# A hybrid two-layer diffusion step on one core: where a group's first weighted sum stands in its tick, and when the second layer's tables are asked for

## The chip, the cores and the metric

The kernel runs on one core of a Trainium2 chip. The metric is the device time of one execution in microseconds (us), the median of several runs. PE is TensorE, DVE VectorE, ACT ScalarE, POOL GpSimd; SP issues the transfers (DMAs).

## The reference

One step of a backbone with two layers over 1024 latent tokens and 256 context tokens of width 1024. What bears on this case:

```python
# layer 0: windowed grouped-query attention (16 heads of 64, 4 key/value heads) beside an mLSTM
q_block: p = softmax([q.k_window + mask, q.k_cache, sink])       # blocks of 128 queries
         o = p_window @ v_window + p_cache @ v_cache
out  = concat(o * silu(za), h_mlstm * silu(zb)) @ w_out_ab
# layer 1: latent attention (16 heads)
qa, kva, kr, z = split(h @ w_in_c)                                # widths 384, 256, 32, 1024
q = rmsnorm(qa) @ w_qb;  kv = concat(rmsnorm(kva), cache_c_kv) @ w_kvb
kr = concat(axial_rope(kr), cache_c_krope)
out = (softmax(q.k) @ v * silu(z)) @ w_out_c
```

Every layer is wrapped in RMSNorm, shift, scale, gate and a residual sum.

## The kernel before

All products run as three float32r matmuls each (high by high, high by low, low by high), so every operand is split by a cast (ACT) and a difference (DVE or POOL). The token axis is cut into 10 tiles of 128 (8 latent, 2 context).

**The windowed attention of layer 0.** `Attention.run` writes the order of the work out by hand, tick by tick, and the engines keep it. The work is 40 groups: 4 key/value heads times 10 query blocks, four query heads each. A group has 2 to 5 blocks of keys, and each block takes one tick of `use`: `turn` transposes the four heads' probabilities on PE into a bank of `mm`, `split` casts them to `att_ph` (ACT) and takes the rest `att_pl` (DVE), and one tick later `weighted` (from line 1041 of the loop) multiplies both with the values into the bank `V`. There is one bank of this kind (`K.set_psum(D=2, mm=3, V=1)`); the first `weighted` of a group (`k == 0`) takes it anew. After the last one, `out` reads it: two ACT instructions (L1145, L1146) and two on DVE (L1147, L1148), all into `att_o`. In the same ticks `scores` computes another group's scores into `D`, `peak` takes their maximum on DVE (L1103, L1104), `exp` the exponentials on ACT (L1109), and `normal` scales them on POOL (L1118).

In between, `extra(i)` fills PE with other work: at first the last projection block, and from tick 26 on steps of the output projection of layer 0 (`out_steps`), three matmuls `mm<-w,o_ah`/`o_al` a step. Up to tick 55 there is a step in every third tick, after that at least one in nearly every tick, sometimes two:

```python
while i > n + 8 and left > (160 - (i - n - 8) / 3 if i < n + 39 else 150 * (A.end - i) / (A.end - n - 39)):
    next(steps)
```

The stretch with a step in every third tick is called the thin part below, the rest the dense part.

**The start of layer 1.** `layer_c` is outside that hand-written order: a scheduler places its instructions on each engine by their dependences. `dense` holds the blocks of the projection `h @ w_in_c`: one block of `z`, two of `u` (the columns of `qa`, `kva` and `kr`), three more of `z`. A block's weights come in four transfers `wf` of two slices each (`DenseBlock.ask`, two buffers), are cast to `wh` (L353, ACT) and subtracted to `wl` (L354, POOL). A `z` block passes each result through `silu2_out` (L644 ACT, L645 DVE into `sz_th`), and SP stores it to `csz`. The `u` results are copied by ACT (L1772). The tables are `rtab` (named `rtabc` in the trace: rotary cosine and sine, 128x2048, 1 MB) and `cc` (the cached latents, 256 and 32 KB): `k_rope` and the later `rope` calls read the first, `k_rope(K, 3)` and transposes after the projection the second. `wq` (2304 KB) is asked for behind `dense.run(2)`.

All transfers stand in one queue, SP's. An issue that waits holds up those behind it.

**The latent attention** (`Mla`) follows, in which POOL forms a small product (L2123) and scales three pieces of the probabilities (L2128) for each block of queries.

Of the kernel before, what the change touches and what calls it, by code (L numbers as in the profile page):

```python
# [143 lines left out]
def body(tc, I, O, dbg=None, stop_at=None):  # L144
    K = Kern(tc, I, O, dbg)
    with ExitStack() as ctx:
        K.const = ctx.enter_context(tc.tile_pool(name="const", bufs=1))
        K.dram = ctx.enter_context(tc.tile_pool(name="dram", bufs=1, space=DRAM))
        K.left = lambda n: tc.alloc_tile_pool(name=n, bufs=1, side="left", reuse_waits="tile")
        K.right = lambda n: tc.alloc_tile_pool(name=n, bufs=1, side="right", reuse_waits="tile")  # L150
        K.set_psum(S=6, T=2)
        setup_consts(K)
        layer_ab(K)
        layer_c(K)
        K.set_psum()
# [176 lines left out]
class DenseBlock:  # L332
# [31 lines left out]
    def run(self):  # L364

        units = self.fn(self.w)
        if self.K.pairs:
            for half in range(2):
                for u in units[0:2]:
                    u.products(half, 2)  # L370
                    yield u.cost / 2
            units = units[2:]
        for u in units:
            n = u.cost if self.K.pairs else 2 * u.cost
            for i in range(n):
                u.products(i, n)
                yield u.cost / n
# [48 lines left out]
class Dense:  # L426
# [30 lines left out]
    def pump(self, now):  # L457

        if not self.blocks:
            return  # L460
        b = self.blocks[0]
        if b.asked < KD // 2 and len(b.wf) < 2:
            b.ask()
            b.when.append(now + 3)
        if b.wf and len(b.w) < 2 * b.bufs - KD and now >= b.when[0]:
            b.when.pop(0)
            b.split()
# [500 lines left out]
class Attention:  # L968
# [51 lines left out]
    def run(self, pump, extra):  # L1020

        K, flow = self.K, self.K.flow
        for i in range(self.end + 5):
            flow.now += 1
            pump(flow.now)
            for f in self.ask.get(i, ()):
                f()
            if i - 2 in self.score:
                G, h = self.score[i - 2]
                if h % 2:  # L1030
                    G.normal(h // 2)
            if i - 1 in self.score:
                G, h = self.score[i - 1]
                G.peak(h)
            if i in self.use:
                G, k = self.use[i]
                G.turn(k)
                G.split(k)
            if i - 1 in self.use:
                G, k = self.use[i - 1]  # L1040
                G.weighted(k)
                if k == len(G.kbs) - 1:
                    G.out()
            if i - 1 in self.score:
                G, h = self.score[i - 1]
                G.exp(h)
            flow.step()
            extra(i)
            if i in self.score:
                G, h = self.score[i]  # L1050
                G.scores(h)
# [777 lines left out]
def layer_c(K):  # L1829
# [10 lines left out]
    K.cc = cu.tile([128, 2, 288], F32, tag="cc", name="cc")  # L1840
    K.u = [cu.tile([128, 672], F32, tag=f"u{t}", name=f"u{t}") for t in range(NT)]
    dense = Dense(K.cblocks)
    dense.run(1)
    K.dma(K.rtab, I["k_ropec"].rearrange("p (a t) -> p a t", a=2))
    K.dma(K.cc[:, :, 0:256], I["cache_c_kv"][0, 0].rearrange("(a p) f -> p a f", p=128))
    K.dma(K.cc[:, :, 256:288], I["cache_c_krope"][0, 0].rearrange("(a p) f -> p a f", p=128))
    ncol = cu.tile([128, 5], F32, tag="ncol", name="ncol")
    ps = K.psT()
    K.tr(ps[:, 0:5], qnr)
# [397 lines left out]
```

## Time and profile before

| | us |
|---|---|
| runs | 2660.78, 2662.75, 2665.32 |
| median | 2662.75 |
| profiled execution, its time | 2661.53 |
| its span, first to last instruction | 2659.5 |
| PE busy | 2584.5 (97%) |
| DVE, ACT, POOL busy | 1775.5, 1409.0, 1167.7 |
| granted PE clock, mean | 0.992 |

The profile is of one execution. A row of a timeline has the start in us from the span's start and the length; what stands in brackets at its end is the engine's idle time before it, with the instruction that ended it. Matmuls overlap, so the length of one is longer than the distance to the next; what the engine really loses at a place is read from starts.

### The profile page before, as it was taken

The page shows a single profiled execution, that of the slowest core. Times are in us where ns is not written, and L with a number is a line of the kernel's source. Part 1 is how long each engine was busy: PE and PEld are TensorE (multiplying, and loading weights), DVE is VectorE, ACT ScalarE, POOL GpSimd, SP SyncE. Part 2 cuts the span into 40 slices and gives each one's busy share as a digit, 9 for nine tenths or more (in the row PEclk, how much of TensorE's full clock was granted, in tenths as well). Part 3 has the DMA queues.
Part 4 walks back from the last instruction along what each step waited for, and adds up shares of the span by engine and source line. Part 5 has one row for each costly group of instructions (what it writes and reads, how often), then busy time and mean ns, then how long its engine had stood idle before and what let it go on. Part 6 is the DMA issues. An engine that isn't in the chain of part 4 may idle for free. (4 is left out here: it accounts for less than half of the span.)

```text
span 2659.5 us, 48212 instructions
## 1 busy us (share of the span) xinstructions
PE 2584.5 (97%) x16209; PEld 2264.8 (85%) x16209; DVE 1775.5 (67%) x4040; ACT 1409.0 (53%) x3598; POOL 1167.7 (44%) x1533
## 2 busy tenths in 40 slices
PE   8989999999999999989999999999999999999998
PEld 6778898898998888877888878987799999999886
DVE  6883565756747566487777545334788888888853
ACT  5222444534533433386666533323688888888842
POOL 5343333523424444275545453223455545555632
PEclk9989999999999999999999999999999999999999
DMA  7555556556657655463433463433311101100333
GB/s 248 177 156 158 161 180 198 170 167 202 203 173 222 204 173 177 150 190 104 129 102 110 128 197 117 132 92 111 104 30 33 39 30 39 37 21 27 123 104 127
DMA packets 344585, 348.79 MB, mean 131 GB/s; under 512 B 29609, under 2 KB 291414, under 8 KB 344082
## 3 DMA queue, kind: packets, MB, share of 16 engines
q1 hardware_dynamic: 344338, 345.71, 42.5%
q8 instruction: 129, 2.11, 0.3%
q14 instruction: 118, 0.97, 0.1%
HBM read 235.09 MB, written 110.51 MB: 130 GB/s over the span
## 5 line engine op out<-in xcount | busy, mean ns | idle before, releaser
L354 POOL TENSOR_TENSOR wl<-wf,wh 128x256 fp32r<-128x256 f32 (+2 forms) x288 | 251.7, 899 | 455.0 <-ACT wh L353 385.1
L103 PE MATMUL mm<-hTh,wh 128*128 128x512 f32 (+1 forms) x912 | 328.3, 360 | 1.6 <-DVE scr L620 0.9
L103 PE MATMUL mm<-hTl,wh 128*128 128x512 f32 (+1 forms) x912 | 325.1, 356 | 0.0
L103 PE MATMUL mm<-hTh,wl 128*128 128x512 f32 (+1 forms) x912 | 325.0, 356 | 0.0
L103 PE MATMUL S<-cK,cQ 96*128 96x512 f32 (+3 forms) x1248 | 297.9, 364 | 3.1 <-ACT cPb L2149 2.0
L2197 DVE TENSOR_TENSOR cpl<-T,cph 128x512 fp32r<-128x512 f32 x336 | 228.4, 685 | 38.8 <-ACT cph L2196 35.2
L103 PEld LDWEIGHTS S<-cK,cQ 96*128 96x128 f32 (+1 forms) x1248 | 192.0, 189 | 26.9 <-ACT cPb L2149 4.8
L2196 ACT CAST cph<-T 128x512 fp32r<-128x512 f32 x336 | 192.6, 590 | 27.6 <-PE T L107 15.3
L103 PEld LDWEIGHTS mm<-hTh,wl 128*128 128x128 f32 x912 | 171.8, 188 | 26.6
L103 PEld LDWEIGHTS mm<-hTh,wh 128*128 128x128 f32 x912 | 171.5, 188 | 25.9 <-DVE bmod L306 1.7
L103 PEld LDWEIGHTS mm<-hTl,wh 128*128 128x128 f32 x912 | 171.6, 188 | 23.1
L2147 DVE TENSOR_REDUCE cmx<-S 128x1 f32<-128x512 f32 x256 | 173.0, 681 | 17.1 <-PE S L103 15.5
L103 PE MATMUL V<-cph,cV 128*128 128x256 f32 x672 | 176.7, 289 | 0.0
L103 PE MATMUL V<-cpl,cV 128*128 128x256 f32 x672 | 172.0, 284 | 1.3 <-DVE cst L2121 1.3
L103 PE MATMUL S<-w,o_ah 128*128 128x512 f32 x492 | 151.8, 395 | 1.7 <-POOL w L820 0.8
L2128 POOL TENSOR_SCALAR cPa<-cPa,cst 128x512 f32<-128x512 f32 x128 | 99.4, 776 | 117.3 <-DVE cst L2125 89.3
L103 PE MATMUL mm<-w,o_ah 128*128 128x512 f32 x468 | 148.6, 396 | 0.0
L1129 ACT CAST att_ph<-mm 128x512 fp32r<-128x512 f32 x168 | 98.6, 587 | 93.8 <-PE mm L107 92.5
L1118 POOL TENSOR_SCALAR att_p<-att_p,att_den 128x640 f32<-128x640 f32 (+1 forms) x128 | 97.5, 775 | 108.9 <-DVE att_den L1115 47.9
L353 ACT CAST wh<-wf 128x256 fp32r<-128x256 f32 (+2 forms) x288 | 102.2, 410 | 70.2 <-DMA wf<-in_w_in_ab 32.4
L1130 DVE TENSOR_TENSOR att_pl<-mm,att_ph 128x512 fp32r<-128x512 f32 x168 | 115.8, 689 | 33.1 <-ACT att_ph L1129 27.9
L103 PE MATMUL mm<-wh,hTh 128*128 128x256 f32 x480 | 135.6, 283 | 0.0
(432 smaller groups left out, 7832.5 us busy)
## 6 DMA issues: line engine op xcount, KB each, us to landing
wf<-in_w_in_ab SPq DMA_DIRECT2D x120, 256.0 KB
in<-in SPq DMA_DIRECT2D x40, 514.0 KB
in<-in SPq DMA_DIRECT2D x32, 386.0 KB
mw<-in_w_mod SPq DMA_DIRECT2D x48, 256.0 KB
in<-scr SPq DMA_DIRECT2D x40, 258.0 KB
o_x<-y SPq DMA_DIRECT2D x20, 512.0 KB
wm<-in_w_mod SPq DMA_DIRECT2D x16, 512.0 KB
in<-cx SPq DMA_DIRECT2D x32, 256.0 KB
```

The costliest lines, as they stand in the source:

```text
L103: return self.nc.tensor.matmul(out, lhsT, rhs, start=start, stop=stop)
L353: K.nc.scalar.copy(wh, wf[:, k])
L354: K.nc.gpsimd.tensor_sub(wl, wf[:, k], wh.bitcast(F32))
L1118: nc.gpsimd.tensor_scalar(pv, pv, den[:, i:i + 1], 1.0, ALU.mult, ALU.mult)
L1129: K.nc.scalar.copy(ph, self.T)
L1130: K.nc.vector.tensor_sub(pl, self.T, ph.bitcast(F32))
L2128: nc.gpsimd.tensor_scalar(pv, pv, wt[:, c:c + 1], rd, ALU.mult, ALU.mult)
L2147: nc.vector.tensor_reduce(mx[:, b, c:c + 1], S, AX.X, ALU.max, negate=True)
L2196: nc.scalar.copy(ph, T_)
L2197: nc.vector.tensor_sub(pl, T_, ph.bitcast(F32))
```

## The change

Two places are written in another order; no instruction is added or removed. In `Attention.run` the `weighted` of a group's first key block is called after `extra(i)` instead of before `exp`. In `layer_c` the three transfers of `rtab` and `cc` are asked for before `dense.run(1)`.

```diff
@@ -1038,7 +1038,8 @@
             if i - 1 in self.use:
                 G, k = self.use[i - 1]
-                G.weighted(k)
+                if k:
+                    G.weighted(k)
                 if k == len(G.kbs) - 1:
                     G.out()
             if i - 1 in self.score:
@@ -1046,6 +1047,10 @@
                 G.exp(h)
             flow.step()
             extra(i)
+            if i - 1 in self.use:
+                G, k = self.use[i - 1]
+                if not k:
+                    G.weighted(k)
             if i in self.score:
                 G, h = self.score[i]
                 G.scores(h)
@@ -1840,10 +1845,10 @@
     dense = Dense(K.cblocks)
-    dense.run(1)
     K.dma(K.rtab, I["k_ropec"].rearrange("p (a t) -> p a t", a=2))
     K.dma(K.cc[:, :, 0:256], I["cache_c_kv"][0, 0].rearrange("(a p) f -> p a f", p=128))
     K.dma(K.cc[:, :, 256:288], I["cache_c_krope"][0, 0].rearrange("(a p) f -> p a f", p=128))
+    dense.run(1)
     ncol = cu.tile([128, 5], F32, tag="ncol", name="ncol")
```

PE at one boundary of the dense part, before: `mm` from `att_p` is a transpose, `V` the weighted sum of the new group, `mm` from `w` a step of the output projection, `D` the scores.

```order
L107 MATMUL mm_16844<-small,att_p_16618 128x128 x2
L107 MATMUL mm_16844<-small,att_p_16679 128x128 x2
L103 MATMUL V_16853<-att_ph_16818,att_v 128x512
L103 MATMUL V_16853<-att_pl_16819,att_v 128x512
L103 MATMUL mm_16638<-w_15377,o_ah_16355 128x512
L103 MATMUL mm_16638<-w_15378,o_ah_16355 128x512
L103 MATMUL mm_16638<-w_15377,o_al_16356 128x512
L103 MATMUL D_16861<-att_kh,att_q_16736 128x384
```

The same place in the changed kernel:

```order
L107 MATMUL mm_16844<-small,att_p_16618 128x128 x2
L107 MATMUL mm_16844<-small,att_p_16679 128x128 x2
L103 MATMUL mm_16638<-w_15377,o_ah_16352 128x512
L103 MATMUL mm_16638<-w_15378,o_ah_16352 128x512
L103 MATMUL mm_16638<-w_15377,o_al_16353 128x512
L103 MATMUL V_16858<-att_ph_16818,att_v 128x512
L103 MATMUL V_16858<-att_pl_16819,att_v 128x512
L103 MATMUL D_16861<-att_kh,att_q_16736 128x384
```

The two matmuls of the first weighted sum have moved behind the three of the step; transposes and scores stand where they were. In a tick without a step nothing moves.

SP's queue at the start of layer 1, before (`csz` are stores of the first `z` block, `mw` weights of the modulation, `bmod` its bias):

```order
L138 DMA kvb<-in_kv_norm_c 128x256
L138 DMA csz_4184_19569<-sz_th_20566 128x512
L138 DMA rtabc<-in_k_ropec 128x2048
L138 DMA csz_4185_19570<-sz_th_20595 128x512
L138 DMA cc<-in_cache_c_kv 128x2x256
L138 DMA cc<-in_cache_c_krope 128x2x32
L138 DMA wq<-in_w_qb_c 128x3x1536
L138 DMA mw_21583<-in_w_mod 128x256
L138 DMA wf_20523<-in_w_in_c 128x2x336
L138 DMA csz_4184_19569<-sz_th_20624 128x512
```

The same place in the changed kernel:

```order
L138 DMA kvb<-in_kv_norm_c 128x256
L138 DMA rtabc<-in_k_ropec 128x2048
L138 DMA cc<-in_cache_c_kv 128x2x256
L138 DMA cc<-in_cache_c_krope 128x2x32
L138 DMA csz_4184_19569<-sz_th_20569 128x512
L138 DMA csz_4185_19570<-sz_th_20598 128x512
L138 DMA wq<-in_w_qb_c 128x3x1536
L138 DMA wf_20526<-in_w_in_c 128x2x336
L138 DMA mw_21583<-in_w_mod 128x256
L138 DMA mw_21585<-in_w_mod 128x256
```

The tables stand ahead of the two stores, and the first `wf` one place ahead of the first `mw`; the third store, which stood right behind `wf`, is now behind `bmod`.

ACT at the same place, before (`wh` casts weights, `sz_th` is the first half of the silu, `u` the copy of a projection result):

```order
L353 CAST wh_20515<-wf_20503 128x336
L353 CAST wh_20519<-wf_20503 128x336
L644 ACTIVATE sz_th_20624<-S_20599 128x512
L353 CAST wh_20525<-wf_20513 128x336
L353 CAST wh_20529<-wf_20513 128x336
L644 ACTIVATE sz_th_20653<-S_20628 128x512
L353 CAST wh_20533<-wf_20523 128x336
L353 CAST wh_20537<-wf_20523 128x336
L644 ACTIVATE sz_th_20682<-S_20657 128x256
```

And in the changed kernel:

```order
L353 CAST wh_20518<-wf_20506 128x336
L353 CAST wh_20522<-wf_20506 128x336
L353 CAST wh_20528<-wf_20516 128x336
L353 CAST wh_20532<-wf_20516 128x336
L644 ACTIVATE sz_th_20627<-S_20602 128x512
L644 ACTIVATE sz_th_20656<-S_20631 128x512
L353 CAST wh_20536<-wf_20526 128x336
L353 CAST wh_20540<-wf_20526 128x336
L353 CAST wh_20727<-wf_20723 128x336
```

The casts have moved ahead of the `sz_th` instructions. Farther on, the scheduler places the first part of the latent attention in a somewhat other order on PE, ACT, DVE and POOL; the rest of it stands as before.

## Rows read from the trace of the kernel before

**Rows 1.** The page's head: span and number of instructions, then busy time of each engine with its share of the span.
```profile
span 2659.5 us, 48212 instructions
...
PE 2584.5 (97%) x16209; PEld 2264.8 (85%) x16209; DVE 1775.5 (67%) x4040; ACT 1409.0 (53%) x3598; POOL 1167.7 (44%) x1533
```

**Rows 2.** TensorE's waits in the dense part of the windowed attention, 1215 to 1510 us: who was waited for, us in total, times, longest.
```profile
PE V L103 <- DVE att_o L1148: 4.8, 20, 0.4
```

**Rows 3.** The same view for the thin part, 1110 to 1215 us.
```profile
PE V L103 <- DVE att_o L1148: 7.4, 9, 1.1
```

**Rows 4.** TensorE in order of time in the dense part: start, length, instruction, out<-in, count, and in brackets the idle time before it with what ended it. The transposes write `mm` from `att_p`, the weighted sum writes `V`, the filling products read `w,o_ah`, the scores write `D`.
```profile
1309.85 0.60 PE L107 MATMUL mm<-small,att_p 128*128 128x128 f32 x4
1310.64 0.47 PE L103 MATMUL V<-att_ph,att_v 128*128 128x512 f32 x1 [0.19 <-DVE att_o L1148]
...
1311.18 0.63 PE L103 MATMUL mm<-w,o_ah 128*128 128x512 f32 x2
...
1311.88 0.34 PE L103 MATMUL D<-att_kh,att_q 128*128 128x384 f32 x1
...
1312.65 0.60 PE L107 MATMUL mm<-small,att_p 128*128 128x128 f32 x4
1313.01 0.48 PE L103 MATMUL V<-att_ph,att_v 128*128 128x512 f32 x1
```

**Rows 5.** TensorE's weight loads in order of time, at the same boundary.
```profile
1310.61 0.19 PEld L103 LDWEIGHTS V<-att_ph,att_v 128*128 128x128 f32 x1 [0.40 <-ACT att_p L1109]
```

**Rows 6.** TensorE in order of time, at a boundary behind the last block of a head group's sequence (narrower windows).
```profile
1299.08 0.60 PE L107 MATMUL mm<-small,att_p 128*128 128x128 f32 x4
1300.05 0.47 PE L103 MATMUL V<-att_ph,att_v 128*128 128x512 f32 x1 [0.36 <-DVE att_o L1148]
```

**Rows 7.** VectorE in order of time, at the boundary of rows 4.
```profile
1310.07 0.43 DVE L1148 SCALAR_TENSOR_TENSOR att_o<-V,att_o 64x256 f32<-64x256 f32 x1
1310.53 0.16 DVE L1103 COPY D<-sink 128x1 f32<-128x1 f32 x1
1310.72 0.82 DVE L1104 TENSOR_REDUCE att_nm<-D 128x1 f32<-128x641 f32 x1
1311.47 0.68 DVE L1130 TENSOR_TENSOR att_pl<-mm,att_ph 128x512 fp32r<-128x512 f32 x1
```

**Rows 8.** TensorE in order of time, at a boundary whose tick before holds two steps of products: the second step of that tick, then transposes and weighted sum of the next.
```profile
1421.90 0.62 PE L103 MATMUL mm<-w,o_ah 128*128 128x512 f32 x2
...
1423.36 0.60 PE L107 MATMUL mm<-small,att_p 128*128 128x128 f32 x4
1423.71 0.48 PE L103 MATMUL V<-att_ph,att_v 128*128 128x512 f32 x1
```

**Rows 9.** TensorE in order of time in the thin part: the weighted sums of two boundaries whose tick holds products.
```profile
1154.62 0.47 PE L103 MATMUL V<-att_ph,att_v 128*128 128x512 f32 x1 [0.91 <-DVE att_o L1148]
...
1185.21 0.47 PE L103 MATMUL V<-att_ph,att_v 128*128 128x512 f32 x1 [0.84 <-DVE att_o L1148]
```

**Rows 10.** TensorE in order of time in the second layer's projection `u` (weights `wh`, `wl`).
```profile
1667.61 0.32 PE L103 MATMUL S<-wl,h1Th 128*128 128x336 f32 x1
1667.76 0.31 PE L103 MATMUL S<-wh,h1Tl 128*128 128x336 f32 x1
1671.27 1.21 PE L103 MATMUL S<-wh,h1Th 128*128 128x336 f32 x3 [3.20 <-ACT wh L353]
...
1675.22 0.48 PE L103 MATMUL S<-wh,h1Tl 128*128 128x336 f32 x1
1675.50 0.48 PE L103 MATMUL S<-wl,h1Th 128*128 128x336 f32 x1
```

**Rows 11.** SP's queue in order of time: start and length of each issue.
```profile
1634.43 0.38 SPq L138 DMA_DIRECT2D kvb<-in_kv_norm_c  x1
1656.33 0.35 SPq L138 DMA_DIRECT2D csz<-sz_th  x1
1656.72 0.43 SPq L138 DMA_DIRECT2D rtabc<-in_k_ropec  x1
...
1659.57 0.48 SPq L138 DMA_DIRECT2D wq<-in_w_qb_c  x1
...
1660.69 0.48 SPq L138 DMA_DIRECT2D wf<-in_w_in_c  x1
...
1669.51 0.26 SPq L138 DMA_DIRECT2D bmod<-in_b_mod  x1
```

**Rows 12.** ScalarE in order of time: the cast of the weights `wf` at the same place.
```profile
1670.75 0.84 ACT L353 CAST wh<-wf 128x336 fp32r<-128x336 f32 x2 [7.21 <-DMA wf<-in_w_in_c]
```

**Rows 13.** The view of transfers, 1656 to 1674 us: GB/s in 40 equal slices (0.45 us each), and the issue of `wq`.
```profile
GB/s 0 0 146 387 323 0 182 328 346 400 346 414 319 387 374 414 441 437 437 396 437 410 410 410 437 437 382 391 341 379 379 410 367 395 383 338 364 391 337 77
...
wq<-in_w_qb_c SPq DMA_DIRECT2D x1, 2304.0 KB
```

**Rows 14.** Busy time by stretch: bounds, length, then PE, PEld, DVE, ACT, POOL busy (with counts), granted clock, DMA share, GB/s.
```profile
1660.00:1680.00 20.00, 16.80 (x91) 16.33 (x90) 8.15 (x16) 4.28 (x10) 5.22 (x6) 0.83 0.93 333
1820.00:1880.00 60.00, 51.07 (x257) 41.10 (x257) 36.41 (x64) 22.24 (x45) 25.54 (x22) 0.89 0.44 143
```

**Rows 15.** The wait of POOL for the block's exponential, in the view of waits over the whole span: us in total, times, longest.
```profile
POOL cst L2123 <- ACT cst L2122: 95.3, 50, 4.4
```

**Rows 16.** POOL's scalings, from the page's groups: count | busy, mean ns of one | idle time before them and what ended most of it.
```profile
L2128 POOL TENSOR_SCALAR cPa<-cPa,cst 128x512 f32<-128x512 f32 x128 | 99.4, 776 | 117.3 <-DVE cst L2125 89.3
```

## The prediction

> **What bounds the kernel now.** The page comes first: TensorE is busy for 97% of the span, the next engine for 67% [rows 1]. So the time moves only where TensorE waits, and I read its waits stage by stage. In the dense part of the windowed attention (1215 to 1510 us) one wait fills the list: the weighted sum on bank `V` waits for `att_o`, 20 times, 4.8 us [rows 2]. In the thin part before it (1110 to 1215 us) the same wait is longer, 9 times, 7.4 us [rows 3]. In the second layer, the longest stop near the edited place is one of 3.2 us at 1671 us, for a cast of projection weights [rows 10, 12]. These are the places that the two edits touch.
>
> **Edit 1: the first weighted sum behind the products.** It removes no instruction. What the sum waits for is the previous group's `out`: two ACT and two DVE passes that read the single `V` bank; the last ends at 1310.50 (1310.07 + 0.43) [rows 7]. TensorE runs in order, so the filling products, the scores and the next transposes are queued behind the waiting sum, and those who wait for the scores (DVE's peak, ACT's exponential) too.
>
> What a wait costs is more than the listed idle. In an ordinary tick the sum starts 0.36 us after the transposes (1312.65 to 1313.01). At the boundary it is 0.79 us (1309.85 to 1310.64): 0.43 lost, 0.19 of it listed [rows 4]. At a boundary after a narrower tick it is 0.97 us (1299.08 to 1300.05): 0.61 lost, 0.36 listed [rows 6]. So each listed wait hides about 0.24 more: 4.8 + 20 x 0.24 = 9.6 us in the dense part. The hidden part is seen in the weight loads: those of the waiting sum start at 1310.61, together with it and not ahead of it [rows 5]. The Trainium skill (TensorE: Matmul & The Clock Gate, the paragraph on engine queue depths in Part 1) says that the engine pulls weight loads ahead of matmuls in flight; by that rule only the listed 4.8 us would be lost and to be won. The trace disagrees at this place, so 9.6 stands.
>
> After the edit three products stand between the transposes and the sum. They take 0.70 us (1311.18 to 1311.88) [rows 4], more than the 0.43 or 0.61 that was lost, so the sum should find its bank free: 0.27 or 0.09 us are left over. The trace of before has a test of that cover. Where the tick before had two steps of products (the first row of the group is its second step), the sum after the boundary starts 0.35 us behind its transposes, no wait [rows 8]. If the cover failed the full 9.6 would stay lost.
>
> What is late next is DVE. In a boundary tick it holds the peak 0.82, the split 0.68, the two passes of `out` at 0.43, plus a small one of 0.16 or two: some 2.6 us, and 1.7 in a tick without `out` [rows 7], against a TensorE tick of 2.37 once the wait is gone (1310.64 to 1313.01) [rows 4]. Over two ticks that is 2.6 + 1.7 = 4.3 against 4.74, so DVE catches up, with little room; where an output tile's own product on DVE falls in as well, some tenths can come back. I take off 0.5 us.
>
> In the thin part most boundary ticks hold no products, and there nothing moves. Two of the nine do have three: 1154.62 and 1185.21 [rows 9]. They stop for over 1 us, so each gains at most the products' 0.70: 1.4 us together.
>
> Edit 1: 9.6 - 0.5 + 1.4 = 10.5 us, bounds 0 and 11.0.
>
> **Edit 2: the tables asked for earlier.** The same three DMAs, 1024, 256 and 32 KB by their shapes, move past two stores on SP's queue. That queue stands idle from 1634.8 to 1656.33, because the first `csz` store waits for its tile; the tables queue behind it, and `wq` (2304 KB) and the first weights `wf` behind them [rows 11]. Moved ahead, the tables are issued and land in that idle stretch, which hides both; no transfer of another kind is asked for there. What gains is the queue behind. `wf` is issued at 1660.69 [rows 11] and ACT casts it only at 1670.75, after a wait for that DMA [rows 12]; TensorE ran out of weights at 1667.9 and restarts at 1671.27 [rows 10].
>
> The price of that stop: start to start 3.51 us instead of 0.15, so 3.35. Behind it the matmuls are 0.28 us apart (1675.22 to 1675.50) instead of 0.15 (1667.61 to 1667.76) [rows 10]; the granted clock of these 20 us is 0.83 [rows 14], that is, the 1.2 GHz level for 6.8 of them (20 x 0.17 / 0.5), after the engine had stood still. Some 0.6 of the 6.8 lie before the restart, as the cast that ends the stop begins at 1670.75 [rows 12]; the other 6.2 are 22 matmuls at 0.28, which would take 3.3 at 0.15: 2.9 lost. Together 6.2 us.
>
> Does `wf` come in time after the edit? Before, `csz`, tables, `csz` and `wq` are 4128 KB, 4.23 MB; at the 0.40 MB/us that the transfer shows in its steady part [rows 13] that is 10.6 us. SP's `bmod`, which stands behind a wait for `wq`, issues at 1669.51 [rows 11], 13.2 us after the first store: 2.6 us of issue and landing. After, 2816 KB are ahead: 7.2 + 2.6 us from 1656.33, so `wq` lands at 1666.1, `wf` (0.34 MB) at 1667.0. TensorE starts 0.52 behind ACT (1670.75 to 1671.27), so at 1667.5; it needs the weights at 1667.9. It fits by 0.4 us. A late landing by 1 us costs about half a us and perhaps no change of clock. ACT's order changes too: the third `sz_th` of the first block now stands behind four casts instead of two (a pair of casts is about 0.85 us), and two `u` copies ahead of the last `sz_th`. TensorE needs the banks that these give back only after 18 to 54 matmuls at 0.15 us. I take 5.5 us, bounds 0 and 6.2.
>
> The built order of the second layer changes also in the first part of the latent attention, not in its rest. I know of no price: zero, with 2 us either way.
>
> **Sum.** The profiled execution took 2661.5 us (span 2659.5), inside the spread of the three runs (2660.8 to 2665.3, median 2662.75). 2661.5 - 10.5 - 5.5 = 2645.5 us, 0.6% below the median. About 0.2% (5.3 us) is what a measurement of this kernel can tell from no change.
>
> **Rivals.**
> - *The stop at 1671 stays, shorter or with its slow clock.* `wq` alone is most of the queue. If the landing slips by 2 us or TensorE stops again at a following bank, edit 2 brings 0 to 2: 2661.5 - 10.5 - 0.5 = 2650.5. For it: the 0.4 us of room. Against: the queue really loses a third of its bytes. The Trainium skill (the same page, HAM oscillation) warns that a pause drops the clock; the half-speed matmuls here agree with it.
> - *The wait at the boundary is handed on.* If DVE, with 2.6 us in such a tick, makes the following scores or splits late, edit 1 keeps only the listed part or less: 2661.5 - 2 - 5.5 = 2654. For it: DVE's load; against: [rows 8], and that DVE has 0.7 us to spare in every other tick.
> - *The second layer gains more.* Clock dips and waits at 1820 to 1880 us (TensorE 51 of 60 us busy, clock 0.89 [rows 14]) depend on when things fall; if some vanish, 5 us more: 2640.
> - *Slower: the rearranged start of the latent attention.* POOL's small product (L2123) is moved ahead of the three scalings (L2128) of the block before at about eight places. There the scalings wait for the product's exponential, 1.9 us on average where it waits now (95.3 / 50), and then take 3 x 0.78 [rows 15, 16]. If TensorE's transposes waited for that, 4.2 us a place and 34 us in all: 2645.5 + 34 = 2679. It decides from 2.7 us a place (2667). Against: at these places others move the other way, and blocks are made several steps ahead of use.
> - *The change does nothing:* excluded for edit 1 by the order of the instructions; 2662 would need both covers to fail.
>
> **Chances.** Forecast (2641 to 2650) 0.70; stop stays 0.13; handed on 0.07; more in the second layer 0.05; slower 0.03; nothing 0.02. The range 2638 to 2655 takes in the first four nearly whole. Faster by over 0.2% (under 2657.4): 0.93; within: 0.04; slower: 0.03.
>
> **What would show it.** Edit 1: the wait of `V` for `att_o` gone from the dense part, transposes to products 0.36 us at boundaries, ticks of 2.37 us; in the thin part seven waits as before. Wrong if new waits on `D` or `att_pl` appear there. Edit 2: tables issued near 1635 on SP's queue, no cast waiting for `wf`, no stop of TensorE near 1671 less what edit 1 moved it, the granted clock 1.00 there. Wrong if `wq` still lands late, or if the time from there to the end grows.

## The result

The changed kernel takes 2645.15 us (median of four runs, 2644.11 to 2648.28) against 2662.44 for the kernel before (2660.78 to 2665.32): a ratio of 0.9936, 95% interval 0.9919 to 0.9953. A second series gave 2644.10 against 2661.54 (0.9933, 0.9918 to 0.9948). The forecast was 2645.5.

The head of the page after; TensorE has lost 11.6 us of busy time with the same 16209 matmuls, since the recorded end of a matmul, which the next one normally overlaps, counts as busy when the next one waits, and a stretch at the lower clock does too. The 11 instructions fewer in the head are waits for semaphores; each engine's own work has the same counts:

```profile
span 2643.0 us, 48201 instructions
...
PE 2572.9 (97%) x16209; PEld 2262.3 (86%) x16209; DVE 1777.3 (67%) x4040; ACT 1406.5 (53%) x3598; POOL 1167.1 (44%) x1533
```

TensorE carries out the same number of matmuls in nearly the same order in both kernels, so the traces can be lined up matmul by matmul. The table gives the length of each stretch (bounded by the start of the matmul with that number), in two traces of each kernel:

| stretch (matmul numbers) | before | before, 2nd | after | after, 2nd |
|---|---|---|---|---|
| to 7000: start, memory part, projections | 1107.98 | 1110.52 | 1108.01 | 1109.87 |
| to 7600: thin part | 103.96 | 103.83 | 102.94 | 103.05 |
| to 9300: dense part | 287.70 | 287.69 | 278.19 | 278.17 |
| to 10050: end of layer 0, first `z` block | 161.09 | 163.69 | 163.09 | 161.82 |
| to 10200: projection `u` | 29.29 | 29.56 | 23.42 | 23.12 |
| 10950 to 11200: start of the latent attention | 58.43 | 58.38 | 56.50 | 56.64 |

The dense part gained 9.5 us, the thin part 0.8 to 1.0, `u` 5.9 to 6.4, the start of the latent attention 1.7 to 1.9 and the matmuls behind it, to some 2070 us, 0.1 to 0.4 more. The first and the fourth row vary by 1.3 to 2.6 us between two executions of one kernel.

**The dense part.** In the view of waits of the changed kernel from 1215 to 1510 us no line is left where [rows 2] had 20 waits. The view of stretches for the two kernels (bounds, length, busy time of PE, PEld, DVE, ACT, POOL, granted clock, DMA share, GB/s), before and then after:

```profile
1211.94:1499.64 287.70, 282.79 (x1702) 236.53 (x1702) 216.83 (x469) 187.54 (x428) 141.79 (x184) 1.00 0.37 108
```
```profile
1210.95:1489.14 278.19, 278.10 (x1702) 236.47 (x1701) 215.59 (x469) 187.27 (x428) 141.90 (x184) 1.00 0.38 112
```

Idle time fell by 4.8 us (287.70 - 282.79 = 4.91 to 0.09), the rest of the 9.5 came out of time listed as busy. Lined up tick by tick, from one group of transposes to the next, the gain stands at 21 boundaries, 0.37 to 0.61 us each; no other tick of this stretch changes by more than 0.08 us. The boundary of [rows 4] in TensorE's order of time, after:

```profile
1305.66 0.60 PE L107 MATMUL mm<-small,att_p 128*128 128x128 f32 x4
1306.02 0.71 PE L103 MATMUL mm<-w,o_ah 128*128 128x512 f32 x2
1306.57 0.40 PE L103 MATMUL mm<-w,o_al 128*128 128x512 f32 x1
1306.81 0.39 PE L103 MATMUL V<-att_ph,att_v 128*128 128x512 f32 x1
```

The products follow the transposes after 0.36 us. VectorE's last pass of `out`, and the weight load of the sum:

```profile
1305.88 0.43 DVE L1153 SCALAR_TENSOR_TENSOR att_o<-V,att_o 64x256 f32<-64x256 f32 x1
```
```profile
1306.57 0.19 PEld L103 LDWEIGHTS V<-att_ph,att_v 128*128 128x128 f32 x1
```

The bank is free at 1306.31, 0.50 us ahead of the sum. The weights are now loaded 0.24 us ahead of it, and in [rows 5] 0.03. That is no sign of the wait: in the undisturbed tick of [rows 4], where the sum at 1313.01 waits for nothing, the load stands 0.03 us ahead of it too. It goes with the place behind the transposes. The kernel before:

```profile
1312.98 0.19 PEld L103 LDWEIGHTS V<-att_ph,att_v 128*128 128x128 f32 x1
```

What the list of waits leaves out can be read from [rows 4]. In the undisturbed tick the transposes are on record to 1313.25 (1312.65 + 0.60), and the sum starts 0.24 us before that. An idle time is counted only from the recorded end on, so each wait there is some 0.24 us longer than listed.

**The thin part.** TensorE's waits from 1110 to 1215 us, after:

```profile
PE V L103 <- DVE att_o L1153: 6.0, 8, 1.3
```

At the two boundaries with products the waits shrank, from 0.91 to 0.18 and from 0.84 to 0.15 (too short for the list), but the boundary right behind the second one waits longer than before. After, and the last of them before:

```profile
1154.61 0.47 PE L103 MATMUL V<-att_ph,att_v 128*128 128x512 f32 x1 [0.18 <-DVE att_o L1153]
...
1189.23 0.47 PE L103 MATMUL V<-att_ph,att_v 128*128 128x512 f32 x1 [1.27 <-DVE att_o L1153]
```
```profile
1190.23 0.47 PE L103 MATMUL V<-att_ph,att_v 128*128 128x512 f32 x1 [1.06 <-DVE att_o L1148]
```

**The projection `u`.** SP's queue after, to set beside [rows 11]:

```profile
1626.93 0.46 SPq L138 DMA_DIRECT2D rtabc<-in_k_ropec  x1
...
1647.83 1.01 SPq L138 DMA_DIRECT2D csz<-sz_th  x2
1648.95 0.40 SPq L138 DMA_DIRECT2D wq<-in_w_qb_c  x1
...
1650.77 0.38 SPq L138 DMA_DIRECT2D wf<-in_w_in_c  x1
```

The tables went out 21 us ahead of the stores. ScalarE's cast of [rows 12], and the stretch of `u` before and after:

```profile
1658.55 0.85 ACT L353 CAST wh<-wf 128x336 fp32r<-128x336 f32 x2 [7.27 <-DMA wf<-in_w_in_c]
```
```profile
1660.73:1690.02 29.29, 26.09 (x153) 25.62 (x152) 16.03 (x35) 5.60 (x13) 4.49 (x5) 0.88 0.80 273
```
```profile
1652.23:1675.65 23.42, 23.39 (x153) 22.91 (x151) 15.69 (x34) 4.80 (x12) 4.28 (x5) 1.00 0.78 267
```

ScalarE still waits for `wf`, but TensorE hardly does: the cast begins 6.3 us behind the first matmul of the stretch (4.8 in the second trace), where it was 10.0 (1670.75 - 1660.73), and the granted clock is 1.00. In the first trace TensorE still loses 0.2 us to POOL's difference `wl` (0.35 from start to start instead of 0.15), in the second nothing.

### The profile page after: what moved, and what is told of

Its sections match the earlier page's. It is cut to its first block, busy times and chain, and to the rows that moved or that the text cites. A ratio compares the mean times of both kernels' runs of the same rounds, so it can differ in the third digit from the quotient of the medians.

```text
span 2643.0 us, 48201 instructions
## 1 busy us (share of the span) xinstructions
PE 2572.9 (97%) x16209; PEld 2262.3 (86%) x16209; DVE 1777.3 (67%) x4040; ACT 1406.5 (53%) x3598; POOL 1167.1 (44%) x1533
## 4 chain that ended last, share of the span: by engine, by line
PE 81%; DVE 6%; DMA 3%; ACT 3%; issue 3%; POOL 2%; SPq 1%; POOLq 0%; DVEq 0%; ACTq 0%
PE mm L103 34%; PE S L103 27%; PE V L103 8%; PE T L107 6%; PE D L103 3%; PE mm L107 2%; SPq L138 1%; PE T L103 1%; DVE macc L321 1%; DVE att_nm L1109 0%; DVE xT L536 0%; ACT att_p L1114 0%; POOL wl L354 0%; DMA o_x<-y 0%; DMA w<-in_w_out_ab 0%
## 5 line engine op out<-in xcount | busy, mean ns | idle before, releaser
L103 PEld LDWEIGHTS mm<-hTl,wh 128*128 128x128 f32 x912 | 171.9, 188 | 22.9
```

The costliest lines, as they stand in the source:

```text
L103: return self.nc.tensor.matmul(out, lhsT, rhs, start=start, stop=stop)
```

## The experiments

**Edit 1 alone.**

The kernel before with this alone:

```diff
-                G.weighted(k)
+                if k:
+                    G.weighted(k)
...
             extra(i)
+            if i - 1 in self.use:
+                G, k = self.use[i - 1]
+                if not k:
+                    G.weighted(k)
```

> Edit 1 alone (first weighted sums behind the products; the tables stay behind the first projection block). The traces of before and after, lined up matmul by matmul, give 11.0 us gained between 1110 and 1502 us, then 2.5 us given back between 1521 and 1651 us, then 5.9 us at the projection u, then 1.6 us in the rest. Theory: the two edits are independent sums of waits. Then this kernel gains 11.0 us by 1502 us, keeps the stop of 3.2 us for the cast of u's weights and the half clock behind it (no gain of 5.9 there), and changes nothing later: about 2651 us if the 2.5 us given back are chance in the transfer of the output weights, about 2653 if they belong to edit 1 (weights that come at a time of their own). Rival: the stop depends on when the attention ends, so it is under 2 us here and the time is 2648 or less.

Measured: 2648.91 us against 2661.08 (0.9954, 0.9941 to 0.9966). The dense part gained 9.5 us, the thin part 1.1. From matmul 9300 to 10050 this execution gained 1.2 where the first trace of after gave back 2.0. The stop is there, 3.04 us, with the clock at 0.94 over the stretch, because less of it ran at 1.2 GHz:

```profile
1664.87 0.73 PE L103 MATMUL S<-wh,h1Th 128*128 128x336 f32 x3 [3.04 <-ACT wh L353]
```
```profile
1654.48:1682.96 28.48, 25.02 (x152) 24.46 (x151) 15.74 (x35) 5.49 (x13) 4.32 (x5) 0.94 0.82 278
```

So the stop does not hang on edit 1, and the 2.0 us "given back" do not come with it.

**Edit 2 alone.**

The kernel before with this alone:

```diff
-    dense.run(1)
     K.dma(K.rtab, I["k_ropec"].rearrange("p (a t) -> p a t", a=2))
...
+    dense.run(1)
```

> Edit 2 alone (tables asked for ahead of the first projection block; first weighted sums where they were). Theory: no change up to the projection u (within 0.3 us), there 5.9 us gained (stop of 3.2 us and half clock gone), 2655.6 us; if the 1.6 us that the changed kernel gains after 1820 us come from the scheduler's other order, which edit 2 alone causes, 2654. Rival: the gains after 1820 us and part of the 5.9 come from the shift by edit 1, and this kernel gains 3 us or less, 2658.5 or more.

Measured: 2658.32 us against 2661.08 (0.9988, 0.9979 to 0.9998). No change in the attention; `u` took 25.67 us, a gain of 3.6 and not 5.9. The long stop is gone and the clock is 1.00, but there are two other waits, the shorter for POOL's difference `wl`, which follows the cast. TensorE's rows of both, and VectorE's rows at the time of the longer one:

```profile
1670.43 0.42 PE L103 MATMUL S<-wl,h1Th 128*128 128x336 f32 x1 [0.44 <-POOL wl L354]
...
1674.60 0.42 PE L103 MATMUL S<-wh,h1Th 128*128 128x336 f32 x1 [1.62 <-DVE sz_th L645]
```
```profile
1669.14 5.07 DVE L321 SCALAR_TENSOR_TENSOR macc<-mw,condT,macc 128x256 f32<-128x256 f32 x6 [0.76 <-DMA mw<-in_w_mod]
1674.13 0.41 DVE L645 SCALAR_TENSOR_TENSOR sz_th<-sz_th,S 128x256 f32<-128x256 f32 x1
```

A bank of the `z` block comes free only when VectorE has worked off six sums of the modulation, which waited for `mw`. VectorE's and TensorE's order in this stretch is the same in the changed kernel; ScalarE's is not. In the changed kernel it copies two `u` results ahead of the last `sz_th`:

```profile
1661.64 0.38 ACT L644 ACTIVATE sz_th<-S 128x256 f32<-128x256 f32 x1
1662.05 0.78 ACT L1777 COPY u<-S 128x336 f32<-128x336 f32 x2
1662.72 0.40 ACT L644 ACTIVATE sz_th<-S 128x256 f32<-128x256 f32 x1
```
```profile
1662.55 0.43 PE L103 MATMUL S<-wh,h1Th 128*128 128x336 f32 x1
```

Here all `u` copies stand behind the last `sz_th`. The kernels with a longer `out` and with moved steps (below) have one `u` copy ahead of the last `sz_th`, and both show the same wait (1.9 us from start to start, as here, against 0.15) and gain 3.6 to 3.7 in this stretch; the one with the sums behind the scores has the order of the changed kernel and no such wait. The matmul that waits is the 66th of the stretch. In both traces of the changed kernel and in the one with the sums behind the scores the same matmul follows the end of the first of those two `u` copies (0.44 us each) by some 0.04 us and has no other wait; in the three kernels with the wait it is VectorE's `sz_th` that it follows by 0.04. So the bank that it takes is freed by ScalarE in the one order and by VectorE in the other, and some 1.7 of the 2.3 us by which edit 2 alone falls short hang on how the scheduler orders ScalarE. The rest goes with the short wait for `wl`, that is, with weights that land some tenths later.

**Only the small table moved.**

On the kernel before:

```diff
+    K.dma(K.cc[:, :, 0:256], ...)
+    K.dma(K.cc[:, :, 256:288], ...)
     dense.run(1)
     K.dma(K.rtab, ...)
-    K.dma(K.cc[:, :, 0:256], ...)
-    K.dma(K.cc[:, :, 256:288], ...)
```

> The kernel before with only the small table (cc, 288 of the 1312 KB) moved ahead of the first projection block; the large one (rtab, 1024 KB) stays behind it. Theory of the bytes: wf comes in late because of what is transferred ahead of it in the one queue. 288 KB are 0.29 MB, at 0.40 MB/us 0.7 us: the stop shrinks from 3.2 to 2.5 us and the half clock stays, so 1 us is gained at the projection, 2660.5 us. Rival: what counts is the order that the scheduler makes of it (the casts ahead of the sz_th on ScalarE, wf's place in the queue), which one moved table is enough to change: the stop is under 1 us and 4 to 6 us are gained, 2656.

Measured: 2661.46 us against 2661.08 (1.0001, 0.9991 to 1.0012), nothing. The stop shrank to 2.47 us, as 0.29 MB less should make it; `u` took 27.47, 1.8 less than before, 0.7 of it from the stop and the rest from less time at 1.2 GHz (clock 0.94):

```profile
1671.15 1.05 PE L103 MATMUL S<-wh,h1Th 128*128 128x336 f32 x3 [2.47 <-ACT wh L353]
```

**wq behind the projection, on the kernel before.**

```diff
-    wq = cu.tile([128, 3, 16, 96], F32, tag="wq", name="wq")
-    K.dma(wq, ...)
...
     dense.run(3, 0.8)
     for _ in dense.mods:
         pass
+    wq = cu.tile([128, 3, 16, 96], F32, tag="wq", name="wq")
+    K.dma(wq, ...)
```

> The kernel before (tables and first weighted sums where they were) with wq (2304 KB) asked for behind the last projection blocks instead of ahead of u's weights. Theory of the bytes: any large transfer taken out of the queue ahead of wf does what the tables did. 2304 KB are 2.36 MB, 5.9 us at 0.40 MB/us, more than the stop of 3.2 us; the cast of u's third pair of weights starts 5 us or more earlier against u's first matmuls, the stop and its half clock go, and the stretch of u takes 23 to 25.7 us against 29.3 and 29.6 in the two traces of before. wq itself is needed only some 130 us later. Time 2655 us. Rival: the tables matter as such, or the order of the casts on ScalarE: the stretch of u stays over 27 us.

Measured: 2656.03 us against 2663.30 (0.9974, 0.9964 to 0.9983). Without touching the tables no matmul of the stretch of `u` starts more than 0.16 us behind the one before it, at full clock:

```profile
1668.06:1691.00 22.94, 22.94 (x153) 22.94 (x152) 12.37 (x27) 5.49 (x13) 4.53 (x5) 1.00 0.90 309
```

With the small table this is a series: 0, 0.29, 1.34 (edit 2) and 2.36 MB taken out of the queue give a stop of 3.2, 2.5, at most 0.4 and none. It is the bytes ahead of `wf`, not the tables. Nor is it the order of ScalarE's casts: this kernel has the order of the kernel before (two casts ahead of the `sz_th`) and no stop, the one with the small table has the order of the changed kernel (four casts) and the stop.

**wq asked for early as well, on the changed kernel.**

```diff
     K.dma(K.cc[:, :, 256:288], ...)
+    wq = cu.tile([128, 3, 16, 96], F32, tag="wq", name="wq")
+    K.dma(wq, ...)
     dense.run(1)
```

> The changed kernel with wq (2304 KB) asked for ahead of the first projection block too, right behind the tables, in the same idle stretch of the queue. Theory: with the tables moved, TensorE has no stop left in u, so weights that come still earlier are worth nothing there: the stretch of u takes 23.4 us as in the changed kernel (25.7 in edit 2 alone, where the scheduler's order leaves a wait of 1.6 us for the last sz_th behind six macc on VectorE that wait for mw, which stand behind wq in the queue), and the time is 2645 us within 2. Rival A: mw comes some 5 us earlier, VectorE's macc with it, and the blocks behind u gain 1 to 3 us, 2643. Rival B: the larger transfer collides with o_x and y of the last output tiles (1625 to 1640 us), TensorE's waits there grow by 1 to 3 us, 2647.

Measured: 2646.25 us against 2661.54 (0.9941, 0.9926 to 0.9956), the same as the changed kernel. The cast that began 6.3 us behind the first matmul of `u` (4.8 in the second trace) now begins with it, and the stretch takes 22.92 us, 0.2 to 0.5 less: weights that come still earlier are worth next to nothing. From matmul 9300 to 10050 it took 2.5 us more than the first trace of before, as much as that of before the second time (2.6), so a collision can't be told from chance: the wait for the cast of the output weights `w` is 1.9 us there, against 0.5 and 0.9 in the two traces of before. `u` has no wait here although its copies stand behind the last `sz_th`, since `mw` too comes some 5 us earlier.

**The sums behind the scores too, on the changed kernel.**

```diff
             extra(i)
+            if i in self.score:
+                G, h = self.score[i]
+                G.scores(h)
             if i - 1 in self.use:
                 G, k = self.use[i - 1]
                 if not k:
                     G.weighted(k)
-            if i in self.score:
-                G, h = self.score[i]
-                G.scores(h)
```

> The changed kernel with the first weighted sum of every group one place farther back, behind the tick's scores as well. In the thin part (1110 to 1215 us), where most boundary ticks hold no products, the scores (some 1.0 us of TensorE) then stand in the wait. Theory: any work of TensorE that is ready covers the wait; the eight listed waits there (6.0 us, and some 0.24 more each that is not listed) fall below 1.5 us in all, the dense part stays without waits, and 5 to 7 us are gained on the changed kernel: 2639 us. Rival: in the thin part VectorE and ScalarE are as full as TensorE (72 of 90 us each against 82), so the wait is handed on to scores' banks and to the rest of the split (waits on D and att_pl appear there of the same size), and less than 2 us are gained: 2643.5 or more.

Measured: 2644.75 us against 2661.08 (0.9935, 0.9922 to 0.9947), no faster than the changed kernel. In the thin part the waits on `att_o` are gone; waits of the scores on their bank `D` stand in their place, 4.6 us where the changed kernel has 0.2:

```profile
PE D L103 <- ACT att_p L1114: 3.3, 4, 1.3
...
PE D L103 <- ACT att_ph L1134: 1.3, 1, 1.3
```

The thin part took 102.42 us against 102.94: of 6.0 us of waits that were taken away 0.5 were gained. There the wait is handed on, as the rival said, though on `D` alone: the waits on `att_pl` are 2.3 us as in the changed kernel.

**Steps on the boundary ticks of the thin part, on the changed kernel.**

```diff
+        thin = (-1 if A.use.get(i - 1, (0, 1))[1] == 0 else 1) if i < n + 39 else 0
-        while i > n + 8 and left > (160 - ...):
+        while i > n + 8 and left > thin + (160 - ...):
```

> The changed kernel with the steps of products in the thin part placed on the boundary ticks instead of every third tick (the number of steps is the same; a step may come one ahead or one late): five boundary ticks that held none now hold one or two. Theory A, the cover: each step hides 0.70 us of a wait of 0.4 to 1.0 listed plus 0.24, and 2.9 us are gained between 1108 and 1212 us on top of the 1.0 of the changed kernel. Theory B, from the kernel with the sums behind the scores (waits on att_o gone in the thin part, but 4.9 us of waits on D and mm in their place, 0.5 us gained): ScalarE and VectorE set the pace there, the wait is handed on, and the gain is under 1 us. I hold B the likelier.

Measured: 2652.11 us against 2663.30 (0.9962, 0.9947 to 0.9977), slower than the changed kernel (0.9936 and 0.9933), and neither theory. The thin part took 4.9 to 5.1 us more. Waits on `att_o` halved to 3.1 us, but the steps came in pairs, and four times TensorE stood at a step whose weights were not split yet:

```profile
PE mm L103 <- POOL w L820: 3.1, 3, 1.2
PE V L103 <- DVE att_o L1153: 3.1, 4, 1.1
...
PE mm L103 <- ACT w L819: 1.3, 1, 1.3
```

So this does not tell what cover is worth in the thin part; the work used as cover was itself not ready. It also lost 2.3 us in `u`, most of it to ScalarE's order, as above.

**A longer `out`, on the changed kernel.**

```diff
+        x = K.t(self.A.ap, [128, 2, 128], F32, "att_x", 1)
+        nc.vector.scalar_tensor_tensor(x[0:64], v[0:64, :, 0, :], 0.5, o[0:64], ALU.mult, ALU.add)
         nc.vector.scalar_tensor_tensor(o[0:64], v[0:64, :, 0, :], 0.5, o[0:64], ALU.mult, ALU.add)
```

> The changed kernel with one pass more on VectorE in every out: the first of its two passes is made once into a scratch tile ahead of them (0.43 us, nobody reads the result), so that the bank V comes free 0.45 us later. In the changed kernel the first weighted sums of the dense part start 0.32 to 1.24 us after the bank is free; 0.15 is the least that occurs where TensorE waits for it, so the room is 0.17 us at four boundaries, 0.25 to 0.4 at eleven or twelve, and 0.85 or more at the others. Theory: the products cover the wait and that is all; once the room is used up, the waits for att_o come back at some 15 boundaries, 0.05 to 0.3 us listed and up to 0.24 more that isn't, 3 to 6 us in the dense part, while the boundaries with two steps stay free. In the thin part each of eight waits grows by 0.45: 3.6 us. Together 2652 to 2655 us. Rival A: the sum has become independent of out, the dense part loses under 0.5 us and the time is 2649 or less. Rival B: VectorE itself is the limit (2.6 + 0.45 + 1.7 = 4.75 us in two ticks of 4.74), so waits on D and att_pl appear in every tick and the dense part loses over 8 us.

Measured: 2655.90 us against 2661.54 (0.9980, 0.9971 to 0.9989), 11.8 more than the changed kernel of the same series. The thin part grew by 5.6 us (3.6 expected), `u` by 2.2 to 2.5 (mostly ScalarE's order again), the dense part by 5.4:

```profile
1217.46:1501.08 283.62, 282.64 (x1701) 234.75 (x1701) 225.52 (x497) 187.61 (x428) 141.86 (x184) 1.00 0.37 109
```

The view of waits lists no wait for `att_o` in the dense part; the idle time before these sums is at most 0.14 us, and that of the whole stretch 1.0 (283.62 - 282.64). Yet the sum stands at the bank's release at every boundary without large room, 0.15 us behind the last pass of `out`. At the boundary where `out` ends at 1314.63, TensorE and its weight load:

```profile
1314.43 0.40 PE L103 MATMUL mm<-w,o_al 128*128 128x512 f32 x1
1314.77 0.47 PE L103 MATMUL V<-att_ph,att_v 128*128 128x512 f32 x1
1315.09 0.40 PE L103 MATMUL V<-att_pl,att_v 128*128 128x512 f32 x1
```
```profile
1314.74 0.19 PEld L103 LDWEIGHTS V<-att_ph,att_v 128*128 128x128 f32 x1 [0.35 <-issue]
```

0.34 and 0.32 us from start to start where the changed kernel has 0.24 and 0.23: 0.2 us lost, none listed. Here place and wait can be told apart: the sum stands behind products in both kernels, and its weight load is 0.24 us ahead of it where the bank is free and 0.03 where it waits. Lined up with the second trace of after, 17 boundaries and the tick behind some of them lose 0.1 to 0.45 us each, 5.5 in all; the boundaries with two steps lose nothing. The theory gave 3 to 6 us, so the cover is a matter of tenths of a microsecond, as the forecast had it.

**Both kernels once more.**

> The changed kernel once more, for a second trace of it. Theory: what belongs to the change recurs: 9.5 us (within 0.3) gained from 1212 to 1500 us, and 23.4 us (within 0.4) for the stretch of the projection u (from the 10050th to the 10200th matmul; 29.3 in the first trace of before). What stands elsewhere in the comparison of the first two traces (2.0 us given back from 1500 to 1661 us, 2.3 us gained between 1832 and 2032 us, 1.1 us given back at 2470 us) is chance of one execution and comes out another way here, by up to 2 us. Rival: those recur too within 0.3 us, and belong to the change.

> The kernel before once more, for a second trace. Theory: the boundaries of the dense part and the stop of about 3 us at the cast of u's weights recur; the half clock behind the stop lasts 3.4 or 6.8 us, so the stretch of u takes 27.5 to 29.3 us; start-up and the stretch from 1500 to 1660 us differ from the first trace by 1 us or more. Rival: the stop was chance of the first execution, and the stretch of u takes under 26 us here.

The stretches are in the table of the result; the single run of before took 2666.21 us. The gains in the attention and in `u` recur. So does the gain at the start of the latent attention (1.7 to 1.8 us), which the theory took for chance. The 1.1 us given back at 2470 us do not recur (0.0), and the fourth row of the table is chance.

## Why the prediction was right, point by point

**Edit 1, dense part.** 9.6 us was worked out, 0.5 taken off for VectorE, 9.5 measured in four kernels. The step that carried it was to count from starts, 0.24 us more for each listed wait than the view of waits shows. The idle time that went was 4.8, just the listed part; the experiment with the longer `out` lost 5.4 us with 0.9 more of idle time.

The reason given for the 0.24 was wrong. It is not seen in the weight loads, which stand 0.03 us ahead of the sum without a wait too (1312.98 and 1313.01); it is the overlap of matmuls on record. So the boundary of [rows 4] did not decide between 4.8 and 9.6 by those loads; the starts did. The Trainium skill (TensorE: Matmul & The Clock Gate, Part 1, Engine queue depths) says that TensorE can pull weight loads ahead of matmuls in flight. The traces agree where the sum stands behind products and its bank is free (load at 1306.57, sum at 1306.81); where it waits there, the load waits with it (1314.74 and 1314.77).

The count was a little lucky too. The prediction's 20 waits leave out two of 0.14 us, too short for the list, and take in one at 1501.84, just behind the stretch of the table; with it the gain is 9.9 us. The room left over was put at 0.27 or 0.09 us; the smallest found is 0.17 (0.32 between the release and the sum, less the 0.15 that occurs when it waits). Next to nothing came back (0.1 us in two ticks), so the 0.5 for VectorE was not needed.

**Edit 1, thin part.** 1.4 us forecast, 0.8 to 1.1 measured: the two covered boundaries gained the 0.7 us each that the products last, and in the ticks behind each of them 0.2 us was given back. The list keeps eight waits there, not seven. The mechanism of the rival "handed on" is real, but lives in the thin part, where the kernel with the sums behind the scores kept 0.5 of 6.0 us.

**Edit 2.** 5.5 us forecast, bounds 0 and 6.2; 5.9 and 6.2 measured against the first trace of before. The price of the stop, 6.2, was right: without one the stretch takes 22.9 us, 6.4 less. The bytes and the rate were right: 0.29 MB less shortened the stop by 0.7 us. The room was as thin as said, but the prediction counted it at the cast and left out POOL's difference `wl` behind it, for which TensorE waits 0.44 us in the kernel with the tables alone and loses 0.2 in the first trace of the changed kernel; the cast itself came 1.5 us earlier in the second. One sign named beforehand did not come: ScalarE's cast still waits for `wf`, 7.27 us. The sentence on ScalarE's order, that TensorE needs the banks later, held in the changed kernel, but it missed what the order is worth: with the `u` copies farther back, 1.8 us are lost to a bank that waits for VectorE's modulation sums, unless `mw` comes earlier too. The prediction didn't look at VectorE there, and so didn't see that the edit's size hung on an order that an edit elsewhere can turn.

**Start of the latent attention.** Zero with 2 us either way; 1.9 to 2.3 gained with the matmuls behind it. In the stretch of the table TensorE was busy for 2.8 us less, with less time at 1.2 GHz (clock 0.94 against 0.88), and idle for 0.9 more:

```profile
1824.82:1883.25 58.43, 49.50 (x252) 40.43 (x251) 38.49 (x67) 24.72 (x49) 28.58 (x27) 0.88 0.49 158
```
```profile
1810.45:1866.95 56.50, 46.69 (x252) 38.81 (x251) 38.02 (x66) 23.27 (x47) 30.36 (x27) 0.94 0.49 159
```

Of six kernels or repeats with both edits five show 1.7 to 2.0 us there and the one with the sums behind the scores 0.1; edit 1 alone shows 0.8, edit 2 alone 1.3, the small table alone 1.5 and `wq` behind the projection nothing. So it can't be put down to one of the edits. The stretch goes with the granted clock: 58.4 us in the three traces at 0.88, 56.9 to 58.5 in the four at 0.91, 56.4 to 56.7 in the five at 0.94. What sets the clock there was not isolated, so this part of the result is not explained. The slower rival (POOL's product ahead of the scalings) did not come.

**The sum.** The stretches give 10.4 + 6.1 + 2.1 = 18.6 us where 16.0 was forecast: 0.4 too little in the dense part, 0.4 to 0.9 in `u`, 2.1 in the latent attention, 0.3 to 0.6 too much in the thin part. The medians differ by 17.3 and 17.4; the rest lies in stretches that vary by up to 2.6 us from one execution to the next. That the forecast met the median within 0.4 us is partly luck: 2.1 us came from a place that was put at nothing, and the profiled execution from which it was counted was 1.2 us under the median of before. Edit 1 alone and edit 2 alone gave 12.2 and 2.8 us by their medians, 2.3 less than both together. That fits the 2.3 us that edit 2 alone lacks in `u`, but each of these gains is uncertain by some 3 us.

## What to carry to other kernels

Where one engine is busy for 97%, read its waits from start to start and compare with an undisturbed place: the list of waits gave half of what the boundary cost, and for a wait of a few tenths nothing. Ready work of the same tick covers such a wait only where the engines behind it have room; in a stretch where they are as full, the wait comes back under another name. For weights that land late, count the bytes ahead in the queue, move the largest transfer that isn't needed yet, and read the scheduled order of every engine again, since it can take back a third of the gain.

## What the runs showed of the hardware

A matmul that finds its bank 0.1 us late costs twice: it starts 0.10 us late, and the next one stands 0.09 us farther off (0.34 and 0.32 us from start to start where 0.24 and 0.23 are usual), while its weight load stands 0.03 us ahead of it instead of 0.24. A stop of 2.5 to 3.4 us of TensorE in `u` was followed by a run at 1.2 GHz each time, of differing length: the granted clock over the stretch was 0.94 in two kernels, which took 27.5 and 28.5 us, and 0.88 in the two traces of before, which took 29.3 and 29.6; where TensorE had no wait it took 22.9. The start differs by up to 5.5 us between executions that have the same matmuls in the same order there (to matmul 5600: 861.4 us in before, 866.9 in edit 1 alone); what makes the difference was not followed.
